# Turning the first layer's queries, keys and probabilities with VectorE's 32x32 blocks and a DRAM scratch instead of TensorE

## The chip, the cores and the metric

The kernel runs on one core of a Trainium2 chip. The metric is the device time of one execution in microseconds (us), as a median of several runs. TensorE (PE) multiplies matrices and writes to PSUM; VectorE (DVE) and ScalarE (ACT) work elementwise; GpSimd (POOL) does small rows here; SyncE (SP) issues nearly all DMAs. Each engine works through its own instructions in order, and waits on semaphores for the others.

## The reference

Two decoder layers over 256 tokens of width 2048, all in float32. The change is in the first layer's token mixer, an attention with 16 heads of width 128. With 256 tokens there is a single key block, so that it is plain causal attention:

```
def moba_attention(h, pos, wq, wk, wv, gq, gk, wo):
    q = rope(rms_norm((h @ wq).reshape(B, S, H, dh), gq), pos, rot)
    k = rope(rms_norm((h @ wk).reshape(B, S, H, dh), gk), pos, rot)
    v = (h @ wv).reshape(B, S, H, dh)
    ...
    s_own = jnp.einsum('bqhd,bhkd->bhqk', qc, k_own).astype(F32) * scale
    s_own = jnp.where(own * BLK + key_off[None, :] <= q_pos[:, None], s_own, NEG_INF)
    p = jax.nn.softmax(jnp.concatenate([s_sel, s_own], axis=-1), axis=-1).astype(v.dtype)
    ...
    return o.reshape(B, S, H * dh) @ wo

for i in range(DEPTH):
    h = rms_norm(x, attn_norm[i])
    y = moba_attention(...) if i == 0 else mla_attention(...)
    x = x + y
    x = x + conv_glu_ffn(rms_norm(x, ffn_norm[i]), ...)
```

The second layer's mixer (`mla_attention`) and both channel mixers (`conv_glu_ffn`) are computed as before the change.

## The kernel before

Every weight is read once from DRAM, 1 MB at a time (a *unit*, tile `raw`, three buffers), and cut into *pieces* of 128 x 512. `Stream.split` (L113) makes two parts of each piece: ACT copies it to a shorter float format (`whi`, L125), and DVE takes the rest (`wlo`, L126). Five buffers hold such parts. A product is then three matmuls: high by high, high by low, low by high.

The program is a list of *quanta*, one for each piece: 1464 in all. The loop at its end (L1199) emits, for quantum q, first the split of the piece four ahead (`ws.split(q + 4)`), then q's matmuls, then whatever is filed under q. Three tables hold that side work: `at` files work behind the quantum, `first_in` files it ahead of that (rank 0 before rank 1), `first` ahead of the quantum itself. The engines' own orders follow from this one order; nothing else schedules.

The first layer has four groups g of four heads. A group is 48 quanta: 16 with pieces of `wq`, 16 of `wk`, 16 of `wv`, each with six matmuls of 128 x 512 (`tok_major`, L254). The results have tokens on the partitions. `plan_heads` (L677) files what follows for queries and for keys, counted from their last quantum q: `evac` from PSUM, squares, the reciprocal root on POOL (`rstd`, q+3), scaling and rotation (q+6 to q+9), and at q+11 the turn: scores need the head's features on the partitions, so `Heads.turned` (L480) transposes each 128 x 128 tile on PE against an identity matrix, eight tiles for the queries and eight for the keys of a group, into PSUM tiles `tp`. `queries_out` and `keys_out` (L643, L652) then cut the turned values into the parts that the score matmuls read.

`Head.plan` (L593) files the four heads. In groups 0 to 2 they come in pairs, six quanta apart; in group 3 singly, two quanta apart. Counted from a head's q0: `scores` on PE and `biased` on DVE (q0), `exps` on ACT (q0+1), `normal` on DVE (q0+2), `turn` on PE, three transposes of the 128 x 384 probabilities `s` (q0+6), `turned` on ACT and DVE right behind it, which makes `pT` and `pT1` out of `tp`; and `values` on PE with `parted` on ACT and DVE (at q0+12, in group 3 about q0+8). After the fourth group, `plan_wo` starts with the output weights; heads 12 to 15 are read there from its 25th quantum on.

Head.plan serves both layers. In the first one `parts` is true.

Of the kernel before, what the change touches and what calls it, by code (L numbers as in the profile page):

```python
# [10 lines left out]
F32 = mybir.dt.float32  # L11
# [3 lines left out]
ALU = mybir.AluOpType  # L15
PSUM = bass.MemoryType.PSUM

P = 128
S = 256
D = 2048  # L20
NT = S // P
# [115 lines left out]
def trunk(ctx: ExitStack, tc: tile.TileContext, a, out):  # L137
    nc = tc.nc
# [5 lines left out]
    ps_acc = ctx.enter_context(tc.tile_pool(name="ps_acc", bufs=4, space=PSUM))  # L144
    ps_tp = ctx.enter_context(tc.tile_pool(name="ps_tp", bufs=2, space=PSUM))
    ps_sc = ctx.enter_context(tc.tile_pool(name="ps_sc", bufs=2, space=PSUM))
    ctx.enter_context(tc.manual_schedule())

    mm = nc.tensor.matmul
# [90 lines left out]
    def at(q, f, *args):  # L240
        side.setdefault(q, []).append((f, args))
# [4 lines left out]
    def first_in(q, rank, f, *args):  # L246
        leading.setdefault(q, [[], []])[rank].append((f, args))
# [133 lines left out]
        nc.sync.dma_start(out[:, j, :], xT[:, j, :])  # L381


    class Heads:


# [65 lines left out]
        def rotate(self, t, stages=range(4)):  # L452
            if not self.rot:
                return
            n, rot = self.n, self.rot
            hf = rot // 2
            tb, C, Sn = self.tabs
            ct = tb[:, C + t * rot : C + (t + 1) * rot]
            st = tb[:, Sn + t * rot : Sn + (t + 1) * rot]
            x = self.x[:, t]  # L460
            def over(s):
                return s[:, None, :].to_broadcast([P, n, s.shape[1]])

            def part(name):
                r = att_pool.tile([P, 16 * 32], F32, name=name, bufs=2)
                return r[:, : n * rot].rearrange("p (n r) -> p n r", n=n)

            if 0 in stages:
                self.rot_parts = part("ro1"), part("ro2")
            t1, t2 = self.rot_parts  # L470
            if 0 in stages:
                nc.vector.tensor_tensor(t1, x[:, :, :rot], over(ct), op=ALU.mult)
            if 1 in stages:
                nc.vector.tensor_tensor(t2[:, :, :hf], x[:, :, hf:rot], over(st[:, :hf]), op=ALU.mult)
            if 2 in stages:
                nc.vector.tensor_tensor(t2[:, :, hf:], x[:, :, :hf], over(st[:, hf:]), op=ALU.mult)
            if 3 in stages:
                nc.vector.tensor_tensor(x[:, :, :rot], t1, t2, op=ALU.add)

        def turned(self, dst, pair, i0):  # L480

            tp = ps_tp.tile([P, 512], F32, name="tp")
            flat = self.x.rearrange("p t n d -> p t (n d)")
            for i in range(2):
                for t in range(NT):
                    c = (i0 + i) * P
                    nc.tensor.transpose(  # L487
                        tp[:, (i * NT + t) * P : (i * NT + t + 1) * P], flat[:, t, c : c + P], ident
                    )
            pair["tp"] = tp  # L490
# [8 lines left out]
    class Head:  # L499
# [32 lines left out]
                mm(second, qr[:, P:], kr[:, part], start=False, stop=part == 1, **flags)  # L532

        def biased(self):
            self.s = att_pool.tile([P, 3 * P], F32, name="s", bufs=3)
            self.st = small.tile([P, 6], F32, name="sst")
            masked = mask
            if self.apart:
                masked = self.s
                nc.vector.tensor_tensor(self.s[:, :P], self.sc[:, 3 * P :], mask[:, :P], op=ALU.add)  # L540
            for c, n, k, m in ((P, S, 1, mask), (0, P, 0, masked)):
                nc.vector.tensor_tensor_reduce(
                    out=self.s[:, c : c + n], in0=self.sc[:, c : c + n], in1=m[:, c : c + n],
                    scale=1.0, scalar=3e38, op0=ALU.add, op1=ALU.min,
                    accum_out=self.st[:, k : k + 1],
                )
# [16 lines left out]
        def turn(self):  # L563
# [2 lines left out]
                nc.tensor.transpose(tp[:, c * P : (c + 1) * P], self.s[:, c * P : (c + 1) * P], ident)  # L566
            self.tp = tp

        def turned(self):

            self.pT = att_pool.tile([P, 2, S], F32R, name="pT", bufs=2)
            self.pT1 = att_pool.tile([P, P], F32, name="pT1", bufs=2)
            hi, lo = self.pT[:, 0], self.pT[:, 1]
            nc.scalar.copy(hi, self.tp[:, :S])
            nc.scalar.copy(self.pT1, self.tp[:, S : 3 * P])
            nc.vector.tensor_tensor(lo, self.tp[:, :S], hi.bitcast(F32), op=ALU.subtract)

        def values(self):
            o = ps_sc.tile([P, 512], F32, name="sc")
# [13 lines left out]
        def plan(self, q, q_values, q_turn=None):  # L593


            q_turn = q_turn or q + 6
            at(q, self.scores)
            at(q, self.biased)

            late = self.rope is not None  # L600
            at(q + 1 + (late and q_turn == q + 6), self.exps)
            at(q + 2 + late + (late and q_turn == q + 6), self.normal)
            first_in(q_turn, 1, self.turn)
            first_in(q_turn, 1, self.turned)
            first_in(q_values, 0, self.values)
            first_in(q_values, 0, self.parted)
# [5 lines left out]
    env = {}  # L612
# [39 lines left out]
    def keys_out(dst, tp, i0, gain=None):  # L652
# [5 lines left out]
        copied(k0[i0 // 2], src[:, :, :P], gain)  # L658
        rest_of(lo, src, hi, gain)

    def evac_parts(state, key, scale):
        v0, v1 = env[key]
        hi, lo = v0[:, 0], v0[:, 1]
        first_, second = (state["acc"][t][:, :512] for t in range(NT))
        if scale is None:
            nc.scalar.copy(hi, first_)
            nc.vector.tensor_tensor(lo, first_, hi.bitcast(F32), op=ALU.subtract)
            nc.scalar.copy(v1, second)
            return
        r = scale()  # L670
        nc.scalar.activation(hi, first_, AF.Copy, scale=r[:, 0:1])
        nc.vector.scalar_tensor_tensor(
            lo, first_, r[:, 0:1], hi.bitcast(F32), op0=ALU.mult, op1=ALU.subtract
        )
        nc.scalar.activation(v1, second, AF.Copy, scale=r[:, 1:2])

    def plan_heads(q, hs, key, out):  # L677

        at(q, hs.evac)
        for t in range(NT):  # L680
            at(q + 1 + t, hs.squares, t)
        at(q + 3, hs.rstd)
        for t in range(NT):
            at(q + 6 + 2 * t, hs.scaled, t)
            at(q + 7 + 2 * t, hs.rotate, t)
        for i0 in (0, 2):
            pair = {}
            q1 = q + 11
            at(q1, lambda hs=hs, p=pair, i0=i0: hs.turned(None, p, i0))
            at(q1, lambda p=pair, i0=i0, key=key: out(env[key], p["tp"], i0))  # L690

    at(-1, n1.scaled, 0)
    def signed_gains():
# [11 lines left out]
    for g in range(4):  # L705
        for kind in "qkv":
            state = {"first": g == 0 and kind == "q"}
            for kt in range(KD):
                q = add(tok_major, state, lambda: n1.h, kt, KD - 1)
                if g == 0 and kind == "q" and kt + 1 < KD:  # L710
                    first(q + 1, n1.scaled, kt + 1)
                if g == 0 and kind == "k" and kt < 12:
                    for j in range(kt * 4 // 3, (kt + 1) * 4 // 3):
                        at(q, n1.square, j)
                        at(q + 1, n1.total, j)
            if g == 0 and kind == "q":
                at(q + 14, n1.sums)
            if kind == "q":
                at(q, moba_tiles, g)
            if kind == "v":  # L720
                at(q, evac_parts, state, ("v", g), lambda: n1.rstd)
                q_v = q
            else:
                hs = Heads(state, 4, P, G_Q if kind == "q" else G_K, 32, (tab, T_MC, T_MS), lambda: n1.rstd)
                plan_heads(q + (0 if g else 15 if kind == "q" else 9), hs, ("qT" if kind == "q" else "kT", g),
                           queries_out if kind == "q" else keys_out)
                q_k = q
        for i in range(4):
            hd = Head(
                4 * g + i, lambda g=g: env["qT", g], lambda g=g: env["kT", g], lambda g=g: env["v", g],  # L730
                i, lambda: env["oT"], parts=True,
            )
            if g < 3:

                q0 = q_k + (14 if g else 22) + i // 2 * 6
                hd.plan(q0, q0 + 12)
            else:
                q0 = q_k + 14 + 2 * i
                hd.plan(q0, max(q0 + 8, q_v + 3 + i))


    def plan_wo(norm, order):
# [301 lines left out]
    class Rotary:  # L1044
# [6 lines left out]
        def out(self, i):  # L1051
            heads = env["qrT"][:, 4 * (self.i0 // 2) + 2 * i : 4 * (self.i0 // 2) + 2 * i + 2]
            tp = self.pair["tp"].rearrange("p (a s) -> p a s", a=2)
            rows, rest = (slice(k * 64, (k + 1) * 64) for k in (i, 1 - i))
            nc.scalar.copy(heads[rows], tp[rows])
            nc.vector.tensor_tensor(heads[rest], tp[rows], heads[rows].bitcast(F32), op=ALU.subtract)
# [263 lines left out]
```

## Time and profile before

| what | value |
|---|---|
| median of 3 runs | 2084.18 us (2083.74 to 2084.41) |
| profiled execution, span from first to last instruction | 2081.8 us |
| what lies around the span (median less span) | 2.4 us |
| granted TensorE clock | 1.000 |
| PE / weight loads / DVE / ACT busy | 2076.9 / 2011.4 / 1415.0 / 1148.0 us |
| DMA | 391.82 MB, 188 GB/s on the mean |

The busy rows say how long an engine had an instruction in work. Matmuls overlap in the pipeline, so the length of a single record is not what the matmul costs: the distance from one start to the next is. DMA issues on SP are not counted as busy; the time to landing is counted from issue to the completion that a waiting engine sees.

The first layer's queries, keys, values and scores fill the span to about 305 us; its output product and channel mixer follow, and then the second layer.

### The profile page before, as it was taken

What the parts mean: (1) busy time and instruction counts of PE and PEld (TensorE: products, weight loads), DVE (VectorE), ACT (ScalarE), POOL (GpSimd) and SP (SyncE); (2) the same over time, 40 slices, a digit from 0 to 9 for tenths busy, and PEclk for the clock granted to TensorE, in tenths of its full rate; (3) what the DMA queues carried; (4) which work ended last, traced back from release to release, by engine and by line L of the source; (5) the groups of instructions that cost most, each with busy time, mean ns of one, the idle gap of its engine ahead of it and who ended that gap; (6) DMA issues with size and microseconds to landing.
All of it is one profiled execution on the core that took longest, in us unless ns stands there. A gap on an engine that the chain in (4) does not pass through costs nothing.

```text
span 2081.8 us, 42114 instructions
## 1 busy us (share of the span) xinstructions
PE 2076.9 (100%) x16742; PEld 2011.4 (97%) x16742; DVE 1415.0 (68%) x2915; ACT 1148.0 (55%) x2248; POOL 46.1 (2%) x36
## 2 busy tenths in 40 slices
PE   9999999999999999999999999999999999999999
PEld 7888889999999999999999889999999999999999
DVE  6877676776666766655556898766667666755554
ACT  6555555555555555555455786655555555544443
POOL 0000000000000000000000110000000000000000
PEclk9999999999999999999999999999999999999999
DMA  7445445555555555555554533555555555555553
GB/s 271 174 173 180 166 162 203 183 193 192 200 187 201 186 199 193 193 202 184 201 194 159 203 124 123 195 190 196 190 202 186 200 189 196 196 198 207 198 205 132
DMA packets 59269, 391.82 MB, mean 188 GB/s; under 512 B 6832, under 2 KB 9520, under 8 KB 13248
## 3 DMA queue, kind: packets, MB, share of 16 engines
q1 hardware_dynamic: 58896, 388.83, 51.7%
q8 instruction: 131, 2.15, 0.4%
q14 instruction: 66, 0.54, 0.1%
q10 hardware_dynamic: 144, 0.26, 0.0%
q0 software_dynamic: 32, 0.04, 0.0%
HBM read 387.01 MB, written 2.10 MB: 187 GB/s over the span
## 4 chain that ended last, share of the span: by engine, by line
PE 100%; DMA 0%; issue 0%; ACT 0%; DVE 0%; POOLq 0%
PE acc L288 26%; PE acc L290 26%; PE acc L289 26%; PE acc L262 18%; PE tp L487 1%; PE tp L566 1%; PE sc L495 0%; PE sc L496 0%; PE sc L494 0%; PE sc L584 0%; PE sc L516 0%; DMA par<-in_par 0%; PE sc L532 0%; PE sc L530 0%; PE tp L357 0%; PE sc L527 0%
## 5 line engine op out<-in xcount | busy, mean ns | idle before, releaser
L126 DVE TENSOR_TENSOR wlo<-raw,whi 128x512 fp32r<-128x512 f32 (+1 forms) x1464 | 996.9, 689 | 375.5 <-ACT whi L125 373.6
L125 ACT CAST whi<-raw 128x512 fp32r<-128x512 f32 (+1 forms) x1463 | 871.2, 620 | 466.9 <-PE acc L289 213.1
L288 PE MATMUL acc<-h,whi 128*128 128x256 f32 x2880 | 795.4, 276 | 0.0
L290 PE MATMUL acc<-h,wlo 128*128 128x256 f32 x2880 | 795.0, 276 | 0.0
L289 PE MATMUL acc<-h,whi 128*128 128x256 f32 x2880 | 794.9, 276 | 0.0
L289 PEld LDWEIGHTS acc<-h,whi 128*128 128x128 f32 x2880 | 540.7, 188 | 0.0
L288 PEld LDWEIGHTS acc<-h,whi 128*128 128x128 f32 x2880 | 540.6, 188 | 0.0
L290 PEld LDWEIGHTS acc<-h,wlo 128*128 128x128 f32 x2880 | 540.6, 188 | 0.0
L288 PE MATMUL acc<-a,whi 128*128 128x256 f32 x1408 | 388.6, 276 | 0.0
L290 PE MATMUL acc<-a,wlo 128*128 128x256 f32 x1408 | 388.6, 276 | 0.0
L289 PE MATMUL acc<-a,whi 128*128 128x256 f32 x1408 | 388.6, 276 | 0.0
L262 PE MATMUL acc<-whi,h 128*128 128x512 f32 (+1 forms) x896 | 268.1, 378 | 0.4 <-ACT h L310 0.4
L289 PEld LDWEIGHTS acc<-a,whi 128*128 128x128 f32 x1408 | 264.3, 188 | 0.0
L290 PEld LDWEIGHTS acc<-a,wlo 128*128 128x128 f32 x1408 | 264.3, 188 | 0.0
L288 PEld LDWEIGHTS acc<-a,whi 128*128 128x128 f32 x1408 | 264.3, 188 | 0.0
L262 PEld LDWEIGHTS acc<-whi,h 128*128 128x128 f32 x896 | 164.8, 188 | 30.3 <-ACT h L310 0.9
L262 PE MATMUL acc<-wlo,h 128*128 128x512 f32 (+1 forms) x448 | 168.4, 376 | 0.0
L288 PE MATMUL acc<-oT,whi 128*128 128x256 f32 x512 | 142.7, 279 | 0.0
L290 PE MATMUL acc<-oT,wlo 128*128 128x256 f32 x512 | 141.6, 277 | 0.0
L289 PE MATMUL acc<-oT,whi 128*128 128x256 f32 x512 | 141.5, 276 | 0.0
L808 DVE TENSOR_TENSOR g<-acc,rstd_b 128x256 f32<-128x256 f32 x88 | 37.5, 426 | 126.0 <-PE acc L290 123.1
L815 ACT ACTIVATE c<-g,par 128x256 f32<-128x256 f32 x88 | 53.1, 603 | 108.0 <-DVE g L808 108.0
(190 smaller groups left out, 1633.7 us busy)
## 6 DMA issues: line engine op xcount, KB each, us to landing
raw<-in_ffn_gu SPq DMA_DIRECT2D x176, 1024.0 KB, 4.8
raw<-in_ffn_down SPq DMA_DIRECT2D x88, 1024.0 KB, 4.8
raw<-in_moba_wk SPq DMA_DIRECT2D x16, 1024.0 KB, 4.8
raw<-in_moba_wv SPq DMA_DIRECT2D x16, 1024.0 KB, 4.8
raw<-in_moba_wo SPq DMA_DIRECT2D x16, 1024.0 KB, 4.8
raw<-in_mla_wo SPq DMA_DIRECT2D x16, 1024.0 KB, 4.8
raw<-in_moba_wq SPq DMA_DIRECT2D x12, 1024.0 KB, 4.8
raw<-in_mla_wkv_a SPq DMA_DIRECT2D x8, 576.0 KB, 3.6
```

The lines of the kernel that those rows point to most:

```text
L125: self.nc.scalar.copy(hi[:, :n], w)
L126: self.nc.vector.tensor_tensor(lo[:, :n], w, hi[:, :n].bitcast(F32), op=ALU.subtract)
L262: mm(state["acc"][t][:, :n], src[:, kt, c : c + P], (t_lo if part == 1 else t_hi)[:, :n], start=kt == 0 and part == 0, stop=kt == k_last a ...
L288: mm(o, w_hi, src[:, kt, :S], start=first and k == 0, stop=False, skip_group_check=True)
L289: mm(o, w_hi, src[:, kt, S:], start=False, stop=False, skip_group_check=True)
L290: mm(o, w_lo, src[:, kt, :S], start=False, stop=kt == k_last, skip_group_check=True)
L487: nc.tensor.transpose(tp[:, (i * NT + t) * P : (i * NT + t + 1) * P], flat[:, t, c : c + P], ident)
L566: nc.tensor.transpose(tp[:, c * P : (c + 1) * P], self.s[:, c * P : (c + 1) * P], ident)
L808: nc.vector.tensor_tensor(self.g[:, 2:], self.gate["acc"][:, :S], self.norm.rstd_b, op=ALU.mult)
L815: nc.scalar.activation(self.c, self.g[:, 2:], AF.Identity, bias=par[:, cb : cb + 1], scale=self.cw(2))
```

## The change

Only the first layer changes. `turned` of queries and keys and `turn` of probabilities are no longer filed. In their place come two steps.

`cross_out`: DVE transposes the 32 x 32 blocks of a tile, each block where it lies (`blk` for queries or keys, two instructions of 128 x 512; `sblk` for one head's probabilities, one of 128 x 384), and SP writes the result to a DRAM tile `there` with four DMAs, one for each 32 partitions. Queries or keys are 512 KB (four DMAs of 128 KB, rows of 1 KB); a head's probabilities are 192 KB (four of 48 KB, rows of 384 bytes). The rows are put down so that blocks change places.

`cross_in`: one DMA, issued by ACT, reads `there` back over the tile that was turned (`qk` or `s`). Its wait is for the four writes. Both steps together transpose the tile.

After that, `crossed_queries` and `crossed_keys` cut the parts as before, out of SBUF and not PSUM, with 32-element runs in their access pattern.

```
+    def cross_out(srcs, b):
+        w = b.shape[1] // P
+        there = dram.tile([4, 32, 4, w * 32], F32, name=f"there{w}")
+        to = b.rearrange("p (j n t c) -> p t n j c", j=4, t=len(srcs), c=32)
+        for t, src in enumerate(srcs):
+            nc.vector.transpose(to[:, t], src.rearrange("p (n j c) -> p n j c", j=4, c=32))
+        for i in range(4):
+            nc.sync.dma_start(
+                there.rearrange("j a i m -> i a j m")[i],
+                b[32 * i : 32 * (i + 1)].rearrange("a (j m) -> a j m", j=4),
+            )
+        return there
+    def cross_in(dst, there):
+        nc.scalar.dma_start(dst, there.rearrange("j a i m -> (j a) (i m)"))
...
-                r = att_pool.tile([P, 16 * 32], F32, name=name, bufs=2)
+                r = att_pool.tile([P, n * rot], F32, name=name, bufs=2)
...
-            self.s = att_pool.tile([P, 3 * P], F32, name="s", bufs=3)
+            self.s = att_pool.tile([P, 3 * P], F32, name="s", bufs=4 if self.parts else 3)
...
+            if self.parts:
+                at(q + 1, self.exps)
+                at(q + 2, self.normal)
+                at(q + 3, self.cross)
+                at(q + 6, self.crossed)
+                first_in(q_values - 2, 1, self.turned)
+                first_in(q_values, 0, self.values)
+                first_in(q_values, 0, self.parted)
+                return
...
+    def crossed_queries(dst, hs):
+        q0, q1 = dst
+        src = hs.heads_of().rearrange("p (n t) i c -> p t n i c", t=NT)
+        hi, lo = (q1[:, part].rearrange("p n (i c) -> p n i c", c=32) for part in range(2))
+        nc.scalar.copy(hi, src[:, 1])
+        nc.vector.tensor_tensor(lo, src[:, 1], hi.bitcast(F32), op=ALU.subtract)
+        nc.scalar.copy(q0.rearrange("p n (i c) -> p n i c", c=32), src[:, 0])
...
-            at(q + 6 + 2 * t, hs.scaled, t)
-            at(q + 7 + 2 * t, hs.rotate, t)
-        for i0 in (0, 2):
-            pair = {}
-            q1 = q + 11
-            at(q1, lambda hs=hs, p=pair, i0=i0: hs.turned(None, p, i0))
-            at(q1, lambda p=pair, i0=i0, key=key: out(env[key], p["tp"], i0))
+            at(q + 5 + 2 * t, hs.scaled, t)
+            at(q + 6 + 2 * t, hs.rotate, t)
+        at(q + 9, hs.cross)
+        at(q + 12, hs.crossed)
+        at(q + 17, lambda: out(env[key], hs))
...
-                q0 = q_k + (14 if g else 22) + i // 2 * 6
-                hd.plan(q0, q0 + 12)
+                q0 = q_k + (19 if g else 28) + i // 2 * 6
+                hd.plan(q0, q0 + 13)
             else:
-                q0 = q_k + 14 + 2 * i
-                hd.plan(q0, max(q0 + 8, q_v + 3 + i))
+                q0 = q_k + 19 + 2 * i
+                hd.plan(q0, q0 + 13)
```

So scaling and rotation come one quantum earlier, the parts of queries and keys six quanta later than before (eight after the blocks are turned), a group's scores five or six later, and the probabilities get 13 quanta from scores to values, instead of 12 or, in group 3, 8. `blk` has one buffer; `sblk` and each kind of `there` have two.

Three places in the engines' orders show it. First PE, where the second pair of heads of group 0 begins (`sc` are the scores, `s` the probabilities of the first pair). Before:

```order
L262 MATMUL acc<-whi,h_149 128x512 x2
L262 MATMUL acc<-wlo,h_149 128x512
L262 MATMUL acc<-whi,h_149 128x512
L566 MATMUL tp<-ident,s 128x128 x6
L516 MATMUL sc<-k_367,q_365 128x128
L494 MATMUL sc<-k,q_366 128x256
L495 MATMUL sc<-k,q_366 128x256
L496 MATMUL sc<-k,q_366 128x256
```

and with the change:

```order
L263 MATMUL acc<-whi,h_150 128x512 x2
L263 MATMUL acc<-wlo,h_150 128x512
L263 MATMUL acc<-whi,h_150 128x512
L547 MATMUL sc<-k_369,q_367 128x128
L525 MATMUL sc<-k,q_368 128x256
L526 MATMUL sc<-k,q_368 128x256
L527 MATMUL sc<-k,q_368 128x256
```

The six transposes are gone, and nothing has come in their place on PE.

Second ACT, in group 1, from the exponentials of the first pair of heads (L550) to the copies of its turned probabilities (L574, L575). Before:

```order
L550 ACTIVATE s,sst<-s,sst 128x128
L550 ACTIVATE s,sst<-s,sst 128x256
L550 ACTIVATE s,sst<-s,sst 128x128
L550 ACTIVATE s,sst<-s,sst 128x256
L125 CAST whi<-raw 128x512
L671 ACTIVATE v<-acc,rstd 128x512
L675 ACTIVATE v_1144<-acc,rstd 128x512
L125 CAST whi<-raw 128x512 x4
L574 CAST pT<-tp 128x256
L575 COPY pT_1732<-tp 128x128
```

With the change, from the pieces behind the same exponentials on (`there_1758` and `there_1765` are the two heads' DRAM tiles, L581 the exponentials of the second pair):

```order
L125 CAST whi<-raw 128x512 x5
L400 DMA s<-there_1758 128x384
L400 DMA s<-there_1765 128x384
L125 CAST whi<-raw 128x512
L581 ACTIVATE s,sst<-s,sst 128x128
L581 ACTIVATE s,sst<-s,sst 128x256
L581 ACTIVATE s,sst<-s,sst 128x128
L581 ACTIVATE s,sst<-s,sst 128x256
L125 CAST whi<-raw 128x512 x4
L619 CAST pT<-s 128x256
L620 COPY pT_1900<-s 128x128
```

Two DMA issues stand between the weight copies, and what stands behind them waits with them: the next weight piece, then the second pair's exponentials, then four more pieces.

Third SP, over the keys of group 1 and the first values. Before there are only weight loads:

```order
L90 DMA raw<-in_moba_wq 128x2048 x4
L90 DMA raw<-in_moba_wk 128x2048 x4
L90 DMA raw<-in_moba_wv 128x2048 x4
L90 DMA raw<-in_moba_wq 128x2048 x4
L90 DMA raw<-in_moba_wk 128x2048 x4
```

and with the change (`sblk` are the heads' blocks, `blk` those of the next queries):

```order
L90 DMA raw<-in_moba_wk 128x2048
L393 DMA there_1758<-sblk 32x4x96 x4
L393 DMA there_1765<-sblk 32x4x96 x4
L90 DMA raw<-in_moba_wk 128x2048
L393 DMA there_1864<-sblk 32x4x96 x4
L393 DMA there_1871<-sblk 32x4x96 x4
L90 DMA raw<-in_moba_wk 128x2048 x2
L90 DMA raw<-in_moba_wv 128x2048
L393 DMA there_2116<-blk 32x4x256 x4
```

The writes stand between the weight loads of the same queue. The program gives its DMAs eight completion counters in turn, over SP and ACT alike, and a DMA waits until the one that had its counter before has landed; so the eighth write of a pair waits for the first to land, and the weight load behind it for the second or third.

More of the change, by code (lines that the diff above doesn't have):

```diff
@@ L146, in trunk @@
     ps_sc = ctx.enter_context(tc.tile_pool(name="ps_sc", bufs=2, space=PSUM))
+    dram = ctx.enter_context(tc.tile_pool(name="dram", bufs=2, space=bass.MemoryType.DRAM))
     ctx.enter_context(tc.manual_schedule())
@@ L464, in part @@
             def part(name):
-                r = att_pool.tile([P, 16 * 32], F32, name=name, bufs=2)
-                return r[:, : n * rot].rearrange("p (n r) -> p n r", n=n)
+                r = att_pool.tile([P, n * rot], F32, name=name, bufs=2)
+                return r.rearrange("p (n r) -> p n r", n=n)
             if 0 in stages:
@@ L478, in rotate, with cross, crossed, heads_of @@
                 nc.vector.tensor_tensor(x[:, :, :rot], t1, t2, op=ALU.add)
+        def cross(self):
+            b = att_pool.tile([P, NT * 4 * P], F32, name="blk", bufs=1)
+            self.there = cross_out([self.x[:, t].rearrange("p n d -> p (n d)") for t in range(NT)], b)
+        def crossed(self):
+            cross_in(self.x.rearrange("p t n d -> p (t n d)"), self.there)
+        def heads_of(self):
+            x = self.x.rearrange("p t n d -> p (t n d)")
+            return x.rearrange("p (i m c) -> p m i c", i=4, c=32)
         def turned(self, dst, pair, i0):
@@ L567, in turn, with cross, crossed @@
             self.tp = tp
+        def cross(self):
+            b = att_pool.tile([P, 3 * P], F32, name="sblk", bufs=2)
+            self.there = cross_out([self.s], b)
+        def crossed(self):
+            cross_in(self.s, self.there)
+            self.tp = self.s.rearrange("p (i n c) -> p n i c", i=4, n=3)
         def turned(self):
@@ L573, in turned @@
             hi, lo = self.pT[:, 0], self.pT[:, 1]
-            nc.scalar.copy(hi, self.tp[:, :S])
-            nc.scalar.copy(self.pT1, self.tp[:, S : 3 * P])
-            nc.vector.tensor_tensor(lo, self.tp[:, :S], hi.bitcast(F32), op=ALU.subtract)
+            if self.parts:
+                hi, lo = (x.rearrange("p (n i c) -> p n i c", n=2, i=4) for x in (hi, lo))
+                first_, second = self.tp[:, :2], self.tp[:, 2]
+                pT1 = self.pT1.rearrange("p (i c) -> p i c", i=4)
+            else:
+                first_, second, pT1 = self.tp[:, :S], self.tp[:, S : 3 * P], self.pT1
+            nc.scalar.copy(hi, first_)
+            nc.scalar.copy(pT1, second)
+            nc.vector.tensor_tensor(lo, first_, hi.bitcast(F32), op=ALU.subtract)
         def values(self):
@@ L598, in plan @@
             at(q, self.biased)
+            if self.parts:
+                at(q + 1, self.exps)
[6 more added lines that the diff above has]
+                return
             late = self.rope is not None
@@ L659, in keys_out, with crossed_keys @@
         rest_of(lo, src, hi, gain)
+    def crossed_queries(dst, hs):
[5 more added lines that the diff above has]
+        nc.scalar.copy(q0.rearrange("p n (i c) -> p n i c", c=32), src[:, 0])
+    def crossed_keys(dst, hs):
+        k0, k = dst
+        for b in range(2):
+            src = hs.heads_of()[:, 4 * b : 4 * b + 4]
+            hi, lo = (k[b][:, part].rearrange("p n (t i c) -> p (n t) i c", t=NT, c=32) for part in range(2))
+            nc.scalar.copy(hi, src)
+            nc.vector.tensor_tensor(lo, src, hi.bitcast(F32), op=ALU.subtract)
+            nc.scalar.copy(k0[b].rearrange("p n (i c) -> p n i c", c=32), src[:, 0::2])
     def evac_parts(state, key, scale):
@@ L725, in trunk @@
                 plan_heads(q + (0 if g else 15 if kind == "q" else 9), hs, ("qT" if kind == "q" else "kT", g),
-                           queries_out if kind == "q" else keys_out)
+                           crossed_queries if kind == "q" else crossed_keys)
                 q_k = q
```

## The prediction

> **What bounds the kernel now.** I read the page's totals and its chain first, then the waits of the first layer's stretch (60 to 290 us), then its busy time by window.
>
> ```profile
> span 2081.8 us, 42114 instructions
> PE 2076.9 (100%) x16742; PEld 2011.4 (97%) x16742; DVE 1415.0 (68%) x2915; ACT 1148.0 (55%) x2248; POOL 46.1 (2%) x36
> PE 100%; DMA 0%; issue 0%; ACT 0%; DVE 0%; POOLq 0%
> ACT whi L125 <- PE acc L262: 35.1, 55, 0.7
> 126.00:193.00 67.00, 67.00 (x331) 56.54 (x330) 48.92 (x151) 37.40 (x85) 3.95 (x2) 1.00 0.49 173
> ```
>
> The reader is to see that PE sets the end alone: it idles 4.9 us in 2081.8, and the chain is PE from start to end. In the first layer ACT's weight copy waits for PE to free a part buffer (55 times), so ACT and DVE run as far ahead as the buffers let them. In the last row, a window over groups 1 and 2, DVE is busy 48.92 us of 67, ACT 37.40, the DMA engines half the time. So whatever leaves PE's queue shortens the run, as long as nothing new makes PE wait.
>
> **What PE loses.** The turns of the first layer by line (up to 300 us; twelve of L566 come later), and PE's timeline around a turn of queries, of two heads, and of one head:
>
> ```profile
> L487 PE MATMUL tp<-ident,qk 128*128 128x128 f32 x64 | 8.3, 272 | 0.0
> L566 PE MATMUL tp<-ident,s 128*128 128x128 f32 x36 | 4.9, 272 | 0.0
> ...
> 62.75 0.39 PE L262 MATMUL acc<-wlo,h 128*128 128x512 f32 x1
> ...
> 64.11 0.39 PE L262 MATMUL acc<-wlo,h 128*128 128x512 f32 x1
> 64.34 0.40 PE L262 MATMUL acc<-whi,h 128*128 128x512 f32 x1
> 64.57 1.04 PE L487 MATMUL tp<-ident,qk 128*128 128x128 f32 x8
> 65.36 0.47 PE L262 MATMUL acc<-whi,h 128*128 128x512 f32 x1
> 65.67 0.39 PE L262 MATMUL acc<-wlo,h 128*128 128x512 f32 x1
> ...
> 92.05 0.82 PE L566 MATMUL tp<-ident,s 128*128 128x128 f32 x6
> 92.70 0.39 PE L516 MATMUL sc<-k,q 128*128 128x128 f32 x2
> ...
> 301.23 0.49 PE L566 MATMUL tp<-ident,s 128*128 128x128 f32 x3
> 301.56 0.39 PE L516 MATMUL sc<-k,q 128*128 128x128 f32 x2
> ```
>
> A piece is six matmuls from one start to the next, 64.11 - 62.75 = 1.36 us. Eight turns hold PE for 65.36 - 64.57 = 0.79 us, and the matmul behind them for 0.08 more (0.31 to the next start, where 0.23 is usual): 0.87. Six cost 0.65, three 0.33. There are 8 turns of queries or keys (64/8), 6 pairs of heads and 4 single ones: 8 x 0.87 + 6 x 0.65 + 4 x 0.33 = **12.2 us** off PE. I count all of it, as the chain has no gap that it could fall into.
>
> [...]
>
> **What DVE and ACT gain and lose.** No row shows a block transpose. The nearest:
>
> ```profile
> L637 DVE TENSOR_TENSOR k<-tp,k 128x512 fp32r<-128x512 f32 x8 | 5.5, 691 | 8.9 <-ACT k L630 8.6
> L558 DVE TENSOR_SCALAR s<-s,sst 128x128 f32<-128x128 f32 (+1 forms) x28 | 7.7, 317 | 0.5
> L434 POOL TENSOR_TENSOR hr<-hms,mhalf 128x8 f32<-128x8 f32 x8 | 15.8, 1978 | 213.1 <-DVE hms L429 213.1
> L106 ACTq DMA_DIRECT2D raw<-in_moba_wq x1: 408/408/408, 0.7 to 0.7; - x1
> ```
>
> By the first, 128x512 takes 0.6 us back to back and 128x384 0.45; if a transpose went at half that rate, twice as much, and at the rate of the second row two thirds. I take 0.6 and 0.45, nearest in size: 16 x 0.6 + 16 x 0.45 = 17 us of DVE over 290 us, which has some 18 us free in each 67. ACT issues 24 reads of 0.41 us, 10 us in all, about what it now spends waiting for PE's turns. The copies behind are as many or fewer, of the same width. Scaling one piece earlier leaves POOL's 1.98 us under 2 pieces of 1.36 us; DVE waits up to 0.9 us more, eight times, in its idle time. All of this costs PE nothing while its cover, four split pieces (5.4 us), holds.
>
> **What the detour adds: waits on ACT's queue.** ACT stands at each `cross_in` until four DRAM writes have landed, and the next weight pieces stand behind it. The landing time L of one write decides. The rows:
>
> ```profile
> L381 SPq DMA_DIRECT2D out<-xT x16: 343/344/347, 1854.6 to 2079.0; - x16
> DMA to landing us min/median/max: 1.7/1.8/3.7
> raw<-in_moba_wk SPq DMA_DIRECT2D x16, 1024.0 KB, 4.8
> raw<-in_mla_wkv_a SPq DMA_DIRECT2D x8, 576.0 KB, 3.6
> xT<-in_xT SPq DMA_DIRECT2D x2, 512.0 KB, 7.1
> par<-in_par SPq DMA_DIRECT2D x1, 176.0 KB, 4.9
> 95.75 0.33 SPq L90 DMA_DIRECT2D raw<-in_moba_wk  x1
> 96.13 0.42 SPq L206 DMA_DIRECT2D par<-in_par  x1
> ```
>
> The stores of the output are 128 KB in rows of 1 KB, issued amid weight loads: 1.8 us, at most 3.7, at 0.34 us an issue. `par`, issued 0.4 us behind a 1 MB load, took 4.9. So L lies between 1.8 and 4.9; I take 2.2, near the stores, as they are writes of this size on this queue.
>
> [...]
>
> Now a pair of heads, on the rows of group 1's first pair:
>
> ```profile
> 146.00 0.28 PE L496 MATMUL sc<-k,q 128*128 128x256 f32 x1
> 146.42 0.40 ACT L550 ACTIVATE s<-s,sst 128x128 f32<-128x128 f32 x1 [1.99 <-DVE sst L542]
> 148.19 0.60 ACT L125 CAST whi<-raw 128x512 fp32r<-128x512 f32 x1
> 148.83 0.69 DVE L126 TENSOR_TENSOR wlo<-raw,whi 128x512 fp32r<-128x512 f32 x1 [1.26 <-ACT whi L125]
> 150.10 0.15 DVE L556 RECIPROCAL sst<-sst 128x2 f32<-128x2 f32 x1
> 151.41 2.50 DVE L126 TENSOR_TENSOR wlo<-raw,whi 128x512 fp32r<-128x512 f32 x4
> ```
>
> Zero is the end of the scores, 146.1. The values' parts, which now lie between 148.83 and 150.10, come three pieces earlier with the change, so the normalizing starts at 3.3 and takes 151.41 - 150.10 = 1.3; one `wlo` later (0.6) DVE has turned the first head at 5.8, the second at 6.2. SP's eight issues, 0.34 apart, end at 8.2, or at 5.8 + L where the eighth waits for the first one's counter. ACT has come to the read at 7.4 (its piece q0+10 waits for piece q0+5) and goes on at R = max(8.2, 5.8 + L) + L + 0.4: 10.6 for L = 2, 16.0 for L = 4.9. PE needs piece q0+11 at 1.36 x 10 and 1.15 for the second pair's scores, 14.8, and ACT and DVE need 1.3 ahead of that: R may be 13.5. So the first read holds PE up from L = 3.7 on.
>
> The second pair is tighter, as its exponentials stand behind that read: they take 1.8, then a piece, 1.3 of normalizing, another piece, and the blocks of its first head are turned at R + 5.9. Its own read ends at R2 = R + 5.9 + max(2.4, L) + L + 0.4. Behind it ACT has a piece, two `oT` copies, the next queries' evacuation (1.25) and piece q0+18, in all 3.65 us to the end of its `wlo`; PE wants that at 17 x 1.36 + 1.15 + 1.2 = 25.5. So R2 may be 21.8. L = 2 gives 21.3, L = 2.2 gives 21.7, L = 3 gives 24.5, L = 4.9 gives 32.1. At my L it just holds.
>
> Group 3 has a head every two pieces and no second pair behind the same read; a read there ends about 6 us after the blocks' quantum begins, and ACT has until 9.5. Queries and keys: the blocks are turned 3.3 us after quantum q+9 begins; issues (1.0), L of 2.2 to 4.9 and ACT's issue make 6.9 to 9.6, and piece q+17 allows 9.6. The read of 512 KB then takes 3.6 (the 576 KB row) to 7.1 (the start of the run, with every queue full), and the keys' parts 2.3: 12.8 to 16.7, where the scores want them at 11 pieces, 15.0. At my L this too holds.
>
> Group 0 is the place where I do charge. Its second pair meets the next queries' squares (8 x 0.21), scaling (2 x 1.1), rotation (2 x 0.8) and blocks (1.2), 6.7 us more of DVE. The 12 pieces from q0+5 on then hold 12 x 0.62 + 1.15 + 1.3 + 0.9 + 0.9 + 0.85 + 6.7 = 19.2 us of DVE in 18.7 of PE, on top of about 2 us in which it waits for ACT at the read. I take **2.5 us**, between 0 and 5.
>
> SP's own lag is harmless: a unit is asked for 8 pieces (10.9 us) ahead of its split and lands in 4.8, and the writes hold SP for 3 to 5 us.
>
> Sum against the profiled execution: 2081.8 - 12.2 + 2.5 = 2072.1 of span. The median of the runs lies 2084.18 - 2081.8 = 2.4 above it: **2074.5 us**.
>
> **Rivals.** First: the reads come late and eat the gain. With L = 3 the second pair costs 24.5 - 21.8 = 2.7 in each of three groups, 8 in all, so 2082; with the keys at their upper end (1.7 in each of four groups) much the same. For it speaks that margins are 0.1 to 1 us by my own sum, and that the 3.7 us maximum occurs among the stores; against it the median of 1.8.
>
> Second, the slower side: writes queue behind the 1 MB loads and land like `par`, in 4.9 us. Then the first pair costs 16.0 - 13.5 = 2.5 and the second 32.1 - 21.8 - 2.5 = 7.8, three times: 31 us, so 2103. The place is `cross_in` on ACT, where a wait stops the weight pieces; it turns the balance from L = 3.4 on, where the stalls reach 12. Against it: the weight load before a pair's writes is issued 3 us or more earlier.
>
> Third: a turn costs PE what its record says, 272 ns, nothing of it lying under its neighbours. Then 112 x 0.272 = 30.5 come off, and 2084.2 - 30.5 + 2.5 = 2056.2. The starts, 0.79 us for eight, speak against it. [...]
>
> **How the numbers follow.** Forecast 0.65, own range 2072 (nothing charged) to 2080; first rival 0.19 (2080 to 2088); second 0.13 (above 2088); third 0.03. A change of 0.2%, 4.2 us, is about what a measurement of this kernel tells from none. Faster: 0.65 + 0.03 = 0.68; within: 0.19; slower: 0.13. The range runs from 2070 to 2090, leaving out the third and most of the second, and takes in L up to 3.4.
>
> **What would show it.** Right: no L487 or L566 turn on PE before 310 us; PE's piece still 1.36 us; writes that land near 2 us; waits of ACT at the reads of 3 to 4 us, after which it catches up; PE's idle time up by some 2 to 3 us, at the second pair of group 0 (110 to 120 us). Wrong: PE waiting for `whi` or `wlo` behind each second pair, near 115, 175 and 248 us (L above 2.2); PE waiting for `k` ahead of the scores; `raw` waited for by ACT; a block transpose above 1 us.

## The result and the profile after

| | before | after |
|---|---|---|
| median | 2084.00 us (2083.74 to 2084.41, 4 runs) | 2103.46 us (2102.28 to 2106.59, 4 runs) |
| profiled execution, span | 2081.8 us | 2100.1 us |
| granted TensorE clock | 1.000 | 0.999 |

The changed kernel takes 1.0096 times as long, with a 95% interval of 1.0082 to 1.0110: slower by about 20 us, where 10 us less were forecast. First the page of the changed kernel: span, busy times and the chain of work.

```profile
span 2100.1 us, 42150 instructions
...
PE 2079.2 (99%) x16630; PEld 1998.6 (95%) x16630; DVE 1428.8 (68%) x2943; ACT 1144.9 (55%) x2240; POOL 45.8 (2%) x36
...
PE 89%; DVE 4%; DMA 3%; ACT 1%; issue 1%; SPq 1%; POOL 1%; ACTq 0%; DVEq 0%; POOLq 0%
```

The chain was all PE; now DVE, DMA, ACT and SP hold 4, 3, 1 and 1% of it. PE has 112 instructions fewer (16630 for 16742), so the turns did go. As they were worth 12.2 us and the span grew by 18.3, some 30 us of waiting must have come in. The waits of the changed kernel up to 340 us (engine, line, what released it: us in total, times, longest) show where:

```profile
ACT whi L125 <- DMA there<-blk: 38.0, 6, 9.1
PEld acc L263 <- DVE wlo L126: 17.8, 34, 1.6
ACT whi L125 <- DMA there<-sblk: 17.1, 3, 7.2
PEld acc L263 <- ACT whi L125: 12.4, 14, 2.3
...
PEld sc L525 <- ACT pT L619: 2.3, 2, 1.3
```

The three PEld rows sum to 32.5 us (1.0 of it stood before the weight pieces in the kernel before too), which is the missing 30. PE waits for weight pieces, and ACT, which makes them, waits for the DRAM writes ahead of its reads, up to 9.1 us at once. The two rows of DRAM writes count nine of the 18 places where ACT reads back. At six more, ACT is idle for 4.8 to 6.5 us until the read has gone out, and the profile puts this down to PE, `par` or DVE, because it names the releaser that came last by its records (186.92 below is one). Next the changed kernel's DMA issues (KB each, median us from issue to landing):

```profile
there<-blk SPq DMA_DIRECT2D x32, 128.0 KB, 2.5
qk<-there ACTq DMA_DIRECT2D x8, 512.0 KB, 4.7
...
there<-sblk SPq DMA_DIRECT2D x64, 48.0 KB, 1.8
s<-there ACTq DMA_DIRECT2D x16, 192.0 KB, 2.9
```

And from the view of the tile `sblk`, the instructions that read and write it (ns, minimum/median/maximum, then first and last start in us):

```profile
L393 SPq DMA_DIRECT2D there<-sblk x64: 303/430/1477, 101.8 to 334.9; - x64
L391 DVE STREAM_TRANSPOSE sblk<-s x16: 534/570/578, 101.2 to 331.6; 128x384 f32<-128x384 f32 x16
```

A write lands in 1.8 to 2.5 us in the median, on both sides of the 2.2 that the prediction took for L: the writes are not slow. But a write's issue holds SP for 0.43 us, not 0.34. Last, group 1's first pair of heads in the changed kernel's timeline (start, length; in brackets the idle time before it and its releaser). The scores end at 160.93.

```profile
166.59 0.62 ACT L125 CAST whi<-raw 128x512 fp32r<-128x512 f32 x1 [0.47 <-PE acc L263]
...
167.12 1.03 DVE L391 STREAM_TRANSPOSE sblk<-s 128x384 f32<-128x384 f32 x2
...
167.72 3.69 SPq L393 DMA_DIRECT2D there<-sblk  x8
...
171.02 3.30 ACTq L400 DMA_DIRECT2D s<-there  x2
...
174.42 0.62 ACT L125 CAST whi<-raw 128x512 fp32r<-128x512 f32 x1 [7.20 <-DMA there<-sblk]
...
175.09 0.19 PEld L263 LDWEIGHTS acc<-whi,h 128*128 128x128 f32 x1 [0.97 <-ACT whi L125]
...
177.36 0.19 PEld L263 LDWEIGHTS acc<-whi,h 128*128 128x128 f32 x1 [0.56 <-ACT whi L125]
...
180.01 0.19 PEld L263 LDWEIGHTS acc<-wlo,h 128*128 128x128 f32 x1 [0.70 <-DVE wlo L126]
...
183.84 2.99 ACTq L400 DMA_DIRECT2D s<-there  x2
...
186.92 0.62 ACT L125 CAST whi<-raw 128x512 fp32r<-128x512 f32 x1 [6.52 <-PE acc L263]
...
187.59 0.19 PEld L263 LDWEIGHTS acc<-whi,h 128*128 128x128 f32 x1 [1.12 <-ACT whi L125]
```

ACT has all buffers full at 166.59 (it waited for PE), then does nothing for the weights from 167.21 to 174.42. Five pieces would have gone past in that time. PE runs dry at 174.4, and again behind the second pair, until 187.6. Between 175 and 182 its weight loads idle 3.6 us in six gaps, not one (by the starts of its matmuls PE falls 3.0 us behind): the exponentials of the second pair stand behind the same read, so the next pieces come late as well.

### The profile page after: what moved, and what is told of

It reads as the page before. It is cut to its first block, busy times and chain, and to the rows that moved or that the text cites. A ratio compares the mean times of both kernels' runs of the same rounds, so it can differ in the third digit from the quotient of the medians.

```text
span 2100.1 us, 42150 instructions
## 1 busy us (share of the span) xinstructions
PE 2079.2 (99%) x16630; PEld 1998.6 (95%) x16630; DVE 1428.8 (68%) x2943; ACT 1144.9 (55%) x2240; POOL 45.8 (2%) x36
## 2 busy tenths in 40 slices
DMA packets 76550, 406.51 MB, mean 194 GB/s; under 512 B 16944, under 2 KB 25776, under 8 KB 30528
## 4 chain that ended last, share of the span: by engine, by line
PE 89%; DVE 4%; DMA 3%; ACT 1%; issue 1%; SPq 1%; POOL 1%; ACTq 0%; DVEq 0%; POOLq 0%
PE acc L289 26%; PE acc L290 26%; PE acc L291 26%; PE acc L263 9%; DVE wlo L126 2%; DMA there<-blk 1%; DMA qk<-there 1%; DVE qk L465 1%; SPq L393 1%; DMA there<-sblk 1%; ACT whi L125 1%; POOL hr L452 0%; DVE blk L391 0%; PE tp L518 0%; DVE junk L428 0%
## 5 line engine op out<-in xcount | busy, mean ns | idle before, releaser
L263 PEld LDWEIGHTS acc<-wlo,h 128*128 128x128 f32 x448 | 84.6, 189 | 31.7 <-DVE wlo L126 17.8
```

Of the source, the lines that this page charges most:

```text
L263: mm(state["acc"][t][:, :n], src[:, kt, c : c + P], (t_lo if part == 1 else t_hi)[:, :n], start=kt == 0 and part == 0, stop=kt == k_last a ...
```

## The experiments

Theories. **A**: ACT stands at the reads, and the weight pieces queued behind them come late. **B**: the block transposes overload DVE. **C**: the new transfers crowd the weight loads, or SP's issues delay them. **D**: the new filing times do harm by themselves. Times are medians; each was measured beside the kernel before on the same chip (2084.0 to 2084.2 us throughout). Where no range stands, it is one run.

### e2: only the new filing

```
-        at(q + 9, hs.cross)
-        at(q + 12, hs.crossed)
-        at(q + 17, lambda: out(env[key], hs))
...
+            at(q + 17, lambda p=pair, i0=i0: hs.turned(None, p, i0))
+            at(q + 17, lambda p=pair, i0=i0: out(env[key], p["tp"], i0))
...
-                at(q + 3, self.cross)
-                at(q + 6, self.crossed)
+                first_in(q_values - 2, 1, self.turn)
```

> The filing times of the changed kernel, but all turns on PE as before: queries and keys turned at q+17, a head's probabilities two quanta ahead of its values. No block transposes, writes or reads. Theories A, B and C: the times alone cost little, 2083 to 2087. Theory D (the later filing brings DVE and ACT work together that did not meet before): 2095 or more.

Measured: 2084.32 us, no change. D falls.

### e5 and e6: e2 with the block transposes, and with the writes too

e5 has the transposes of `cross` beside PE's turns, their results unused; e6 has the 96 writes as well, and no read.

```
+        at(q + 9, hs.cross)
...
+                at(q + 3, self.cross)
```

> All turns on PE at the changed filing times, and besides the block transposes of DVE into tiles that nobody reads; no writes, no reads. Theory B (DVE's added 17 to 20 us delay wlo): 2095 or more. Theories A and C: within 3 us of the kernel with the shifted times alone.

> As the kernel with block transposes alone, plus SP's 96 writes to DRAM; nothing is read back, and the turns are PE's. Theory C, or SP's queue held up by the writes (weight loads late): 5 us or more above the kernel with block transposes alone. Theory A: within 3 us of it, as ACT has nothing to wait for.

Measured: 2084.25 and 2084.13 us. Some 19 us of DVE, 7 MB of writes (32 x 128 KB and 64 x 48 KB) and 41 us of SP's issues (96 x 0.43), by the rows of the changed kernel, cost nothing. B falls, and C for the writes.

### e3 and e4: only the probabilities, only queries and keys

e3 takes the diff of e2 for queries and keys alone, e4 for the probabilities alone; what is not taken back goes through DRAM as in the change.

> The changed kernel with queries and keys turned on PE (at q+17); only the probabilities go through DRAM. By the gaps of the changed kernel's trace (theory A), the pairs hold about 18 of 31 us; with 7.0 us of turns back on PE and 5.2 saved: 2084 - 5.2 + 18 = 2097, down to 2090 if a pair's late start came from late keys. Theory B: half of the added DVE work is gone, so half of the loss: about 2091. Theory C: 6.3 of 14.7 MB remain: about 2092.

> The changed kernel with the probabilities turned on PE (two quanta ahead of the values); only queries and keys go through DRAM. By the gaps of the trace (theory A), queries and keys hold about 13 of 31 us: 2084 - 7.0 + 13 = 2090. Theory B: about 2091. Theory C: 8.4 of 14.7 MB: about 2094. If the gaps of the two kinds only arise together, 2078 to 2082.

Measured: 2092.29 and 2088.87 us, 8 and 5 above before. Each half loses, and together they lose more than the sum of both, 20 instead of 13. Both rest on one run each; the differences are far above the 1.1 us by which runs of before differ, though runs of the changed kernel spread over 4.3. By the times expected, these two do not tell A from B and C; e5 and e6 do.

### e1: the reads on POOL

```
-        nc.scalar.dma_start(dst, there.rearrange("j a i m -> (j a) (i m)"))
+        nc.gpsimd.dma_start(dst, there.rearrange("j a i m -> (j a) (i m)"))
```

> The change, with the reads back issued from POOL's queue and not from ACT's; nothing else differs. Theory A (ACT stands at the reads until the writes have landed, and the weight pieces behind it come late): the stand moves to POOL, which has 46 us of work in all; ACT's waits for there<-blk and there<-sblk (55 us in the changed kernel) vanish and PE's gaps shrink from about 31 us to under 5, so 2072 to 2078. Theory B (DVE has too much: 16 block transposes of 0.69 us and 16 of 0.57 us delay wlo): gaps stay, about 2100. Theory C (writes and reads crowd the weight loads, whose landing went from 4.8 to 5.2-5.9 us): gaps stay, about 2100. D (the later filing of scores and values): about 2100.

Measured: 2105.35 us (2101.15 to 2108.63), ratio 1.0103 (1.0086 to 1.0120). A miss for A as it was put. The waits up to 340 us say why:

```profile
ACT k L730 <- DMA qk<-there: 20.7, 4, 6.3
...
ACT q L720 <- DMA qk<-there: 15.5, 4, 5.5
...
PEld sc L547 <- ACT k L732: 12.7, 4, 4.5
```

ACT no longer stands at the reads; it stands at their results, the `crossed_keys` and `crossed_queries` copies (L730, L720), which were filed five quanta behind the read. From POOL's queue a read took 6.6 us (`qk`) and 5.2 (`s`) to land; the stand has moved, and PE waits for the keys.

### e7: the reads on ACT, two quanta later

```
-                at(q + 6, self.crossed)
+                at(q + 8, self.crossed)
...
-        at(q + 12, hs.crossed)
+        at(q + 14, hs.crossed)
```

> The changed kernel with each read filed two quanta later (q0+8 and q+14) on ACT, all else in place. Theory A: ACT comes to a read 2.7 us later, so of waits of 5 to 7 us some 2.7 go; PE's gaps fall by half or more, 2080 to 2090, unless the keys' read (4.7 us to landing, parts wanted at q+17) now makes ACT wait there. Theories B and C: about 2100.

Measured: 2100.95 us, far above the 2080 to 2090 of A; the exception that the expectation named came true, ACT waiting for the keys' read. Its waits up to 340 us:

```profile
ACT q L720 <- DMA qk<-there: 16.1, 4, 5.0
ACT pT L619 <- DMA s<-there: 15.9, 8, 3.4
ACT k L730 <- DMA qk<-there: 15.5, 4, 4.4
...
ACT whi L125 <- DMA there<-blk: 8.1, 3, 3.3
```

The stand at the writes shrank from 38.0 to 8.1 us (`blk`), and ACT stands 47 us at the results, where it stood 5 in the changed kernel. Part of this is that the reads landed later: 7.3 us (`qk`) and 5.0 (`s`) in the median, 4.7 and 2.9 in the changed kernel. Why they did isn't shown. So A needs a second half: ACT stands wherever the round trip is shorter in the program than on the chip, at the read or at its user.

### e8: the reads on SP, one quantum behind the writes

```
-        nc.scalar.dma_start(dst, there.rearrange("j a i m -> (j a) (i m)"))
+        nc.sync.dma_start(dst, there.rearrange("j a i m -> (j a) (i m)"))
...
-                at(q + 6, self.crossed)
+                at(q + 4, self.crossed)
...
-        at(q + 12, hs.crossed)
+        at(q + 10, hs.crossed)
```

> The changed kernel with the reads issued from SP's queue, filed one quantum behind the writes; ACT waits for no write any more. Theory A: ACT's waits vanish; SP stands instead for about 3 us at each read, and the weight loads behind it, which are asked for 10.9 us ahead and land in 5 to 6, still come in time: 2072 to 2080. Theory C: about 2100, or worse, as the weight loads come later still.

Measured: 2082.32 us, far below the 2100 of C and just above the 2072 to 2080 of A. Its waits up to 340 us:

```profile
ACT k L730 <- DMA qk<-there: 10.9, 4, 3.5
...
PEld acc L263 <- DVE wlo L126: 10.4, 25, 1.2
...
ACT pT L619 <- DMA s<-there: 3.6, 3, 2.0
...
PEld sc L547 <- ACT k L732: 2.9, 4, 1.3
```

SP may stand at a read, as its next weight load was asked for 8 pieces (10.9 us) ahead and landed in 5.2 to 6.4 us in the median. What is left are ACT's shorter waits for the results, 10.9 us at keys, 3.6 at probabilities and (in the row left out) 7.3 at queries, and 13.3 us of PE's gaps in the two PEld rows.

### e9: ACT's reads as in the change, their results unused

PE's turns feed the parts (as in e2), `cross` and `crossed` run at their places, and the read goes back into the block tile.

```
-            cross_in(self.x.rearrange("p t n d -> p (t n d)"), self.there)
+            cross_in(self.b, self.there)
...
-            cross_in(self.s, self.there)
+            cross_in(self.b, self.there)
```

> The 112 turns stay on PE, at the changed kernel's filing times, and feed the parts. Beside them everything of the detour runs: block transposes, the 96 writes, and the 24 reads on ACT at their places, but a read puts its tile back into the block tile, and nothing uses it. So ACT stands at the reads as in the changed kernel, and no part waits for a read to land. If the loss is ACT's standing at the read with weight pieces behind it: PE gaps before the weight pieces nearly as in the changed kernel (30 us there, less up to 1 us at each of the 18 places, where the turn on PE gives that much more lead), so 2102 to 2114 us. If the loss is only that the turned data arrive after their filed time: 2084 to 2088. About half of each: 2090 to 2100.

Measured: 2107.34 us (2106.68 to 2110.02), ratio 1.0114 (1.0101 to 1.0128). The waits up to 340 us:

```profile
ACT whi L125 <- DMA there<-blk: 48.4, 8, 8.5
...
ACT whi L125 <- DMA there<-sblk: 17.2, 3, 6.5
PEld acc L263 <- DVE wlo L126: 12.8, 23, 1.2
PEld acc L263 <- ACT whi L125: 12.3, 16, 2.3
```

Against e6 the only thing added is 24 reads on ACT whose results nobody needs (only the block tile's next use comes behind them), and they cost 23 us (2107.34 - 2084.13), with the gaps in the same two rows as in the changed kernel. The stand at the read is enough for the loss.

### e10: e8, and the users later

```
-        at(q + 17, lambda: out(env[key], hs))
+        at(q + 19, lambda: out(env[key], hs))
...
-                q0 = q_k + (19 if g else 28) + i // 2 * 6
-                hd.plan(q0, q0 + 13)
+                q0 = q_k + (21 if g else 30) + i // 2 * 6
+                hd.plan(q0, q0 + 14)
...
-                q0 = q_k + 19 + 2 * i
+                q0 = q_k + 21 + 2 * i
```

> The reads on SP, one quantum behind the writes (as in e8), and the users filed later: parts of queries and keys two quanta, scores two quanta, a head's values 14 instead of 13 quanta behind its scores in groups 0 to 2. If what e8 still loses is the data's lateness (ACT 10.9 us at keys, 7.3 at queries, 3.6 at probabilities, and the wlo behind them), these waits go to nearly nothing, no PE wait for k before the scores is left, and only gaps from crowded DVE quanta remain: 2072 to 2078 us. If the remaining loss is the transfers crowding the weight loads, or DVE's blocks, it stays at 2080 to 2085 whatever the filing.

Measured: 2074.70 us (2074.68 to 2075.16, 5 runs), ratio 0.9956 (0.9942 to 0.9969): faster than both kernels. Its page, span and chain:

```profile
span 2072.7 us, 42119 instructions
...
PE 97%; DVE 2%; DMA 1%; issue 0%; POOL 0%; ACT 0%; SPq 0%; DVEq 0%; ACTq 0%
```

The gaps of 0.2 us and more in its timeline of PE's weight loads from 40 to 320 us:

```profile
80.33 0.19 PEld L263 LDWEIGHTS acc<-wlo,h 128*128 128x128 f32 x1 [0.78 <-DVE wlo L126]
...
112.50 0.19 PEld L263 LDWEIGHTS acc<-wlo,h 128*128 128x128 f32 x1 [1.34 <-DVE wlo L126]
...
116.03 0.19 PEld L526 LDWEIGHTS sc<-pT,v 128*128 128x128 f32 x1 [0.88 <-DVE pT L621]
```

Three gaps are left, 3.0 us, all in group 0, where DVE has the most to do (in the changed kernel it is busy 16.5 of the 20 us from 100 to 120, and 10.2 to 14.3 of the 20 us from 148, 168 and 240 on). 2081.8 - 12.2 + 3.0 = 2072.6 is the span to 0.1 us. This kernel moves the same bytes as the changed one (406.51 MB), reads included, so C falls for the reads too.

### e11 and e12: the reads on ACT, the users later

e11 is e7 with the users of e10; e12 is the changed kernel with the users of e10.

> Reads on ACT, two quanta later than in the changed kernel (as in e7), and the users as late as in e10. If ACT's standing is only a matter of time, so that a read filed late enough finds the writes landed: the waits on the writes stay at e7's 10 us in all, the users' waits of e7 (16 us at q, 16 at pT, 15 at k) shrink to under 10, and the time is 2076 to 2086. If the read must leave ACT's queue, whatever its time: above 2090.

> Reads on ACT where the change has them, and only the users as late as in e10. If the stand at the read makes the loss, as e9 says: nothing gained by later users, 2098 to 2106, with PE's gaps before weight pieces where the changed kernel has them. If e10 was fast because of its later users: 2074 to 2080.

Measured: 2082.21 us (2081.91 to 2083.76), ratio 0.9992 (0.9983 to 1.0002), and 2099.62 us (2099.17 to 2100.85), ratio 1.0077 (1.0060 to 1.0094). With e7, e8 and e10 they make a table:

| reads filed | users as in the change | users later |
|---|---|---|
| on ACT, q0+6 and q+12 (the change) | 2103.46 | 2099.62 (e12) |
| on ACT, q0+8 and q+14 | 2100.95 (e7) | 2082.21 (e11) |
| on SP, q0+4 and q+10 | 2082.32 (e8) | 2074.70 (e10) |

Time alone for the users brings 4 us, time alone for the reads 3 (one run, and within the spread of the changed kernel's own runs), both together 21: ACT stands at whichever of the two comes too early. Moving the read to SP, where it can be filed right behind the writes, brings 21 without later users and 29 with them.

## Why the prediction was wrong, step by step

**The turns, 12.2 us: right.** e10 has no turn on PE and the whole detour, and its span is 9.1 us shorter with 3.0 us of gaps. So the third rival (272 ns a turn, 2056) falls: (9.1 + 3.0) / 112 is 0.11 us a turn.

**DVE, 2.5 us in group 0: right, as far as e10 shows.** Its three gaps are 3.0 us, 2.2 of them at 112 and 116 us, where the second pair was charged, and 0.8 at the queries. The block transposes take 0.69 us (128 x 512) and 0.57 (128 x 384), where 0.6 and 0.45 were taken as back-to-back costs; back to back they cost 0.64 and 0.52 (1.29 and 1.03 us for two, first start to last end halved). With the turns still on PE they cost nothing (e5, 2084.25 us).

**The forecast's own number was the time of another kernel.** 2074.5 us was the sum without any stall at the reads. That is e10, at 2074.70; that both agree to 0.2 us is partly luck, as e10's filing differs.

**The step that failed** is "At my L it just holds", and its like for queries and keys, "At my L this too holds": the stands of ACT at `cross_in` were charged at nothing. They and what stands behind them make up some 27 of the 30 us of waiting: 3.0 are left in e10, where ACT stands neither at the reads nor, but for 2 us, at their results. It was not L alone that did it. Three terms of the sum were too small, the limits were one piece too late, and the limits asked for too little:

- *DVE gets there later.* The second head of group 1's first pair is turned at 168.15, 7.2 us behind the scores, not 6.2. For the keys the blocks are done 4.4 us after quantum q+9 began, not 3.3: `scaled` (L465) waits 0.9 us for POOL, and two blocks take 1.3.
- *The issues.* Eight take 3.69 us on SP, 0.46 each. The eighth starts at 171.0, 10.0 us behind the scores, where 8.2 was worked out. In the trace it has the counter of the first write (semaphore 116 for both), which had landed by 170.4, so that it did not wait for that one.
- *The last landing.* ACT's second read goes out at 174.0, 3.0 us behind the last write's issue, though the median of such writes is 1.8. So R is 174.4 - 160.9 = 13.5 us, where the sum gave 10.8: 1.0 from DVE, 0.8 from the issues, 0.8 from the landing. For the keys of group 1 it is 9.0 (4.4 + 1.8 + 2.5 + 0.3) instead of 6.9, by the rows below.
- *The limits, one piece too late.* The prediction let R be 13.5, because PE would first want piece q0+11 behind the read. But the bound that `split` is given is exclusive, so `ws.split(q + 4)` ends with piece q+3: the newest piece lies three ahead of the quantum, not four, and the first piece behind the read is q0+10.

```
AHEAD_PIECES = 4
...
        while self.split_to < min(upto, len(self.pieces)):
...
        ws.split(q + min(1 + q // 6, AHEAD_PIECES))
```

  The trace agrees. Behind the first scores PE did nine pieces and the second pair's scores (9 x 1.36 + 1.15 = 13.4) and was dry 13.45 us behind them, at 174.38; the copy of the next piece began at 174.42. So R may be 12.1 and not 13.5, R2 20.4 and not 21.8, and a read of queries or keys may end 8.2 us after q+9 began and not 9.6. By these limits the prediction's own R2, 21.7, is 1.3 us late at L = 2.2 already; in three groups that is 4 us. The rest comes from the terms above and from what follows.
- *What stands behind the read.* The limit asked only when the next piece must be ready. But ACT's 1.8 us of exponentials and DVE's 1.3 of normalizing and 1.0 of blocks fall upon the pieces behind it, which have no cushion left: the gaps at 177 to 182 us. In group 2 the first read ended 11.4 us behind the scores (the next piece's copy began at 251.98), within 12.1. There PE had no gap at the piece behind the read, and yet it waited 1.3 us in three gaps for the `wlo` of later pieces (0.35, 0.69 and 0.30, at 255.66, 257.58 and 259.11). In group 1 the second pair's R2 is then about 26.0, and PE waits again.

The keys of group 1 in the changed kernel's timeline (their quantum q+9 began at 143.90), then group 2's first pair (its scores ended at 240.55):

```profile
148.30 1.78 SPq L393 DMA_DIRECT2D there<-blk  x4
...
152.56 0.33 ACTq L400 DMA_DIRECT2D qk<-there  x1
...
152.99 2.18 ACT L125 CAST whi<-raw 128x512 fp32r<-128x512 f32 x4 [5.54 <-DMA there<-blk]
...
153.66 0.19 PEld L263 LDWEIGHTS acc<-whi,h 128*128 128x128 f32 x1 [0.50 <-ACT whi L125]
...
257.58 0.19 PEld L263 LDWEIGHTS acc<-wlo,h 128*128 128x128 f32 x1 [0.69 <-DVE wlo L126]
```

Four pieces, all the lead there is, are cut in one go behind the keys' read. PE wanted the first of them, q+16, at 143.90 + 7 x 1.36 = 153.42. So a read that ended at 9.0, within the 9.6 of the prediction, still made PE's weight loads wait for `whi` (0.50 us) and then for `wlo` (0.54).

The second rival named the place (`cross_in` on ACT stops the weight pieces), and its 2103 is the time measured. But its cause, writes that land in 4.9 us, isn't what happened: 1.8 and 2.5 are the medians. Its break-even, L = 3.4, was too high by the same missing terms and the same piece. The first rival had the cause nearer (margins of 0.1 to 1 us) and the size too small, 8 us.

**Covers that held.** SP's lag did no harm that the times show (e6 at 2084.13 us, and e10 at 2074.70 with the reads on SP itself). The writes of 384-byte rows landed sooner than those of 1 KB rows (1.8 against 2.5 us in the median, at 48 and 128 KB). One reading was off, though nothing of the sum hangs on it: from 60 to 290 us ACT waited 27.4 us for PE's turns before the change (10.2 at keys, 9.9 at queries, 7.3 at probabilities), not the 10 that the prediction set against its issues.

What stays open: why each half's loss adds up to less than the whole (8 + 5 against 20), beyond the author's estimate, which no run shows by itself, that a stand that meets a pipe without lead costs in full; and how much of e1 comes from its slower landing and how much from POOL's order, since in that kernel POOL's other work stands in the same queue (some 7 us of it are PE's clock, see below).

## What to carry to other kernels

A DMA that reads back what was just written was here, on the queue of an engine that computes, a wait of that engine for the whole chain ahead of it (last producer, all issues, last landing): 13.5 us behind the scores, where 12.1 were allowed. Put it on a queue whose next work is asked for early (e8: 21 us less), and file its user behind the second landing, not the first (e10: 7.6 less again). Price such a wait with the latest write (here 3.0 us, for a median of 1.8) and the duration of the issue itself (0.46, for 0.34), and hold it against the lead that is left when everything queued behind it has also been served, not only the next item. Count that lead in the loop that makes it, with its bounds: here it was one piece shorter than its name. Where a sum "just holds" with margins of a few tenths at twenty places, the likely case is that it doesn't.

## What the runs showed of the hardware that was not expected

PE's granted clock fell to half, from 1.00 to 0.50, after pauses. In the kernel with the reads on POOL (e1), PE stood from 158.0 to 162.2; the windows (length, busy us of PE, weight loads, DVE, ACT and POOL, then the granted clock, DMA share, GB/s; x counts the instructions that touch the window):

```profile
159.00:160.00 1.00, 0.00 (x0) 0.00 (x0) 0.00 (x0) 0.00 (x0) 0.00 (x0) 1.00 1.02 430
160.00:161.00 1.00, 0.00 (x0) 0.00 (x0) 0.00 (x0) 0.00 (x0) 0.00 (x0) 0.56 0.69 291
161.00:162.00 1.00, 0.00 (x0) 0.00 (x0) 0.18 (x1) 0.83 (x2) 0.00 (x0) 0.50 0.14 57
...
166.00:167.00 1.00, 1.00 (x4) 0.73 (x4) 0.49 (x1) 1.00 (x5) 0.00 (x0) 0.53 0.00 0
167.00:168.00 1.00, 1.00 (x6) 0.82 (x5) 0.24 (x1) 1.00 (x4) 0.00 (x0) 1.00 0.00 0
```

The clock was 0.50 from about 160.1 to 166.9, so that for 4.7 us after the pause PE ran at half its pace: the weight loads of its matmuls of 128 x 512 start 0.43 us apart there (two at 164.45 and 164.88), where 0.23 is usual. In the changed kernel it happened once while PE had work, behind pauses of 1.39 and 0.22 us at 208 to 211 us:

```profile
211.00:212.00 1.00, 1.00 (x5) 0.77 (x4) 1.00 (x3) 0.98 (x2) 0.00 (x0) 0.57 0.75 266
212.00:213.00 1.00, 1.00 (x4) 0.81 (x3) 0.31 (x1) 0.41 (x2) 0.00 (x0) 0.50 0.67 238
...
214.00:215.00 1.00, 1.00 (x4) 0.73 (x4) 1.00 (x2) 1.00 (x3) 0.00 (x0) 0.72 0.89 369
```

Half the clock for some 3.4 us cost it an estimated 1.6 us beyond the gap (eight matmuls that start 0.43 us apart and not 0.23). The six short gaps between 175 and 182 us had no such effect, and neither had PE's longest pause in that kernel, 1.84 us up to 88.78: the clock stayed at 1.00 behind it. So a pause can cost more than its length, and its length alone doesn't tell whether it does. In e1 (mean clock 0.996) it happened four times and in e7 (0.997) three times; an estimate of what this cost PE is 7 and 5 us, half of the 15 and 10 us over which its weight loads took 0.33 us and not 0.19.
